# Windowed attention and a conformer layer on one Trainium2 core: half pages for the low parts of the output weights, and probability tiles in a pool of their own

## The chip, the cores and the metric

The kernel runs on one core of one Trainium2 chip. The metric is device time in microseconds (us) of one execution. The engines are named as the profile names them: PE (matrix multiply), DVE (vector), ACT (activation), POOL (GpSimd) and SP (the queue from which most DMAs are issued).

## The reference

Two layers on 1024 tokens of width 1024, with 256 context tokens, all in fp32. Layer A is windowed attention with a sink, layer B a conformer convolution. The change lies in the attention of layer A:

```python
for i in range(DEPTH):                       # 0: attention, 1: conformer convolution
    shift, scale, gate = split(silu(c) @ ada_w[i] + ada_b[i])
    h = rmsnorm(x, norm_g[i]) * (1 + scale) + shift
    if i % 2 == 0:
        q, k, v, z = split(h @ w_in)         # 16 q heads, 4 k/v heads of 128; q, k rotated
        kc, vc = split(h_ctx @ w_in[:, q_end:v_end])
        # per head and block of 128 queries: 3 blocks of 128 keys, 256 context keys, a sink
        s = concat([sink, q @ kc.T, q @ k_window.T]) * HEAD_DIM ** -0.5
        p = softmax(s)
        o = p_ctx @ vc + p_win @ v_window
        y = (o * silu(z)) @ w_out
    else:
        y = conformer_conv_branch(h, ...)    # GLU, depthwise conv of 31, layernorm, swish, gate
    x = x + gate * y
return rmsnorm(x, final_g)
```

## The kernel before, in words

Every fp32 operand of a matrix product is held as a high part (rounded to the matmul format) and a low part (the rest), and a product is three matmuls: high by high, low by high, high by low. ACT makes the high part by a copy, DVE or POOL the low part by a subtraction (`split_lo`). Names end in `h`/`hi` and `l`/`lo`.

Memory on the chip is 45 pages of 1024 words per partition and 6 half pages of 528 words (class `Pages`). A page is taken from the head of a list of free pages and put back at its end, so each tile lands on whichever page came free longest ago. The first instruction that writes a page's new tile waits for the last users of the old one.

The program is written as one sequence; a scheduler then sets the order of each engine's instructions by simulating them. PE's instructions are kept in program order from the start of attention. All compute instructions are issued through one helper (`InOrder.call`), so the profile shows them all on line L90 (in the listing of the changed kernel the same helper is L102).

Attention is a list of 128 steps, (h, qb) for 16 heads and 8 blocks of queries; step i = 8h + qb. In one step PE does: `scores` of step i+2 (into PSUM tile `pss`), some 11 to 15 matmuls of projections as filling (`fill`, PSUM tile `psg`), at some steps `pv` (into `pso`), and the `transposes` of step i (again a `pss`). Around them:

- `scores(h, qb)`: POOL copies the sink (`nsink`) into one column of a probability tile `p`, DVE adds the mask and takes the maximum in one custom instruction (`p<-pss,mask,nsink`, shown as CUSTOM_DVE_ANT_0 in the profile and ISA in an order), ACT takes the exponential, DVE the reciprocal, POOL scales. `p` is a whole page and three are live at a time.
- `transposes(h, qb)`: ACT copies the transposed probabilities to `pthi`, DVE subtracts to get `ptlo`; both are single tiles that `pv` reads after every fourth step.
- The projections' weights come through `WStream`: a load to `wraw` on SP, `whi` on ACT, `wlo` mostly on DVE. The rotation of q and k (`rope_start`, `rope_end`) multiplies by cosine and sine, and swaps the two halves of the head with two DMAs in between (on SP at the start of attention, on ACT later). At the start of attention (the code ahead of `steps`) rotated tiles of the first heads, the context's k and v (`kvc`) and the first `scores` overlap.
- `low_parts()`: the low parts of the two output weights (Wo of attention, Wp of layer B) are made once and stored to DRAM (`wolA`, `wolC`) for later. Before: 32 items of 512 KB on a page, each in three calls (load; first half: `lhi` on ACT into a half page, subtraction on POOL in place; second half likewise, then a store), one call per step.
- `adag` streams rows of the modulation weights (`dww_raw`, `wsum_raw`) which DVE accumulates into `mask_page`.
- At step (15,1) of the program the out-projection begins (the scheduler places parts of it earlier): loads of the attention's output `ozf` and of `wo` and `wol` through SP, split into `ozh`, `ozl`, `woh` on ACT and DVE.
- After heads 3, 7 and 11 the k and v of the next group are made between two steps ("regroup").

## Time and profile before

| | us |
|---|---|
| three runs of the kernel | 1745.61, 1746.29, 1748.8 |
| their median | 1746.29 |
| profiled execution, its own time | 1744.99 |
| its span, first to last instruction | 1743.2 |
| PE busy in the span | 1723.9 |
| DVE busy | 1151.1 |
| ACT busy | 868.2 |
| POOL busy | 853.5 |

The profiled execution is one more execution than the three runs; it is 1.3 us below their median, and its time is 1.8 us over its span. PE is busy in 99% of the span. So the views to read are those that show the few stretches in which PE waits, and what the other engines do in them: the list of PE's waits, then timelines of single engines there. Attention runs from 94.88 us (first `scores`) to some 840 us.

### The profile page before, as it was taken

What the parts mean: (1) busy time and instruction counts of PE and PEld (TensorE: products, weight loads), DVE (VectorE), ACT (ScalarE), POOL (GpSimd) and SP (SyncE); (2) the same over time, 40 slices, a digit from 0 to 9 for tenths busy, and PEclk for the clock granted to TensorE, in tenths of its full rate; (3) what the DMA queues carried; (4) which work ended last, traced back from release to release, by engine and by line L of the source; (5) the groups of instructions that cost most, each with busy time, mean ns of one, the idle gap of its engine ahead of it and who ended that gap; (6) DMA issues with size and microseconds to landing.
All of it is one profiled execution on the core that took longest, in us unless ns stands there. A gap on an engine that the chain in (4) does not pass through costs nothing.

```text
span 1743.2 us, 23901 instructions
## 1 busy us (share of the span) xinstructions
PE 1723.9 (99%) x8471; PEld 1424.9 (82%) x8471; DVE 1151.1 (66%) x2094; ACT 868.2 (50%) x1417; POOL 853.5 (49%) x797
## 2 busy tenths in 40 slices
PE   9999999999999999999999999999999999999998
PEld 5788888888888888887888888888888888887886
DVE  4676663666366654556215189999999999877912
ACT  5544443455344543446234355664665564466731
POOL 0135553655355543552001267998898888131410
PEclk9999999999999999999999999999999999999999
DMA  9334533454335443437776723020121202377971
GB/s 316 110 85 138 155 120 93 134 158 136 88 119 159 153 140 94 121 107 262 247 254 220 251 85 97 13 61 25 46 76 37 91 31 79 121 264 243 325 260 49
DMA packets 195324, 242.46 MB, mean 139 GB/s; under 512 B 11798, under 2 KB 126790, under 8 KB 195204
## 3 DMA queue, kind: packets, MB, share of 16 engines
q1 hardware_dynamic: 188692, 230.81, 40.6%
q10 hardware_dynamic: 6512, 10.11, 2.5%
q8 instruction: 67, 1.10, 0.3%
q14 instruction: 53, 0.43, 0.1%
HBM read 188.70 MB, written 41.69 MB: 132 GB/s over the span
## 4 chain that ended last, share of the span: by engine, by line
PE 91%; DMA 3%; DVE 3%; ACT 1%; issue 1%; POOL 1%; ACTq 0%; SPq 0%; DVEq 0%; POOLq 0%
PE psg L90 46%; PE pss L90 23%; PE pso L90 22%; DMA rope_half<-rope_half 1%; POOL rope_half L90 1%; DVE mask_page L90 1%; DVE ptlo L90 0%; DMA wo_page<-in_conv_w_out_dram 0%; DMA ozf_page<-ozd 0%; DMA wsum_raw<-in_ada_w_dram 0%; DMA wolC<-low_page 0%; DMA low_page<-in_conv_w_out_dram 0%; DVE p_page L90 0%; DVE x_page L90 0%; DMA rope_page<-rope_page 0%
## 5 line engine op out<-in xcount | busy, mean ns | idle before, releaser
L90 POOL TENSOR_TENSOR odd_half<-odd_half,prod_half 128x513 f32<-128x513 f32 (+2 forms) x252 | 313.2, 1251 | 23.8 <-ACT prod_half L90 10.5
L90 PE MATMUL psg<-hh_page,whi_page 128*128 128x512 f32 x608 | 240.7, 396 | 0.2 <-DVE kvc_page L90 0.2
L90 PE MATMUL psg<-hh_page,wlo_page 128*128 128x512 f32 x608 | 239.7, 394 | 0.0
L90 PE MATMUL psg<-hl_page,whi_page 128*128 128x512 f32 x608 | 239.4, 394 | 0.0
L90 ACT ACTIVATE prod_half<-ubuf,dww 128x513 f32<-128x513 f32 (+2 forms) x252 | 165.1, 674 | 110.6 <-POOL odd_half L90 108.4
L90 POOL TENSOR_SCALAR p_page<-p_page,sc 128x640 f32<-128x640 f32 (+1 forms) x128 | 109.3, 854 | 178.4 <-DVE sc L90 177.2
L90 PE MATMUL psg<-h2h_page,whi_page 128*128 128x512 f32 x464 | 183.8, 396 | 0.0
L90 PE MATMUL psg<-h2l_page,whi_page 128*128 128x512 f32 x464 | 182.5, 393 | 0.0
L90 PE MATMUL psg<-h2h_page,wlo_page 128*128 128x512 f32 x464 | 182.5, 393 | 0.0
L90 DVE SCALAR_TENSOR_TENSOR pss<-ubuf,dww,pss 128x512 f32<-128x512 f32 (+3 forms) x270 | 172.4, 671 | 0.1
L90 DVE SCALAR_TENSOR_TENSOR pss<-ubuf,wsum,pss 128x512 f32<-128x512 f32 (+3 forms) x270 | 171.8, 671 | 0.2
L90 ACT ACTIVATE p_page<-p_page,sc 128x641 f32<-128x641 f32 (+1 forms) x128 | 103.1, 806 | 129.9 <-DVE sc L90 114.9
L90 DVE TENSOR_TENSOR ptlo<-pss,pthi 128x640 fp32r<-128x640 f32 (+1 forms) x144 | 103.1, 716 | 62.0 <-ACT pthi L90 61.6
L90 ACT ACTIVATE pthi<-pss 128x640 fp32r<-128x640 f32 (+1 forms) x144 | 88.9, 617 | 103.4 <-PE pss L90 95.2
L90 PEld LDWEIGHTS psg<-hh_page,wlo_page 128*128 128x128 f32 x608 | 114.2, 188 | 24.0
L90 PEld LDWEIGHTS psg<-hh_page,whi_page 128*128 128x128 f32 x608 | 114.3, 188 | 23.0 <-DVE kvc_page L90 0.4
L90 PEld LDWEIGHTS psg<-hl_page,whi_page 128*128 128x128 f32 x608 | 114.3, 188 | 21.4
L90 POOL TENSOR_TENSOR wlo_page<-wraw_page,whi_page 128x1024 fp32r<-128x1024 f32 x35 | 87.9, 2514 | 86.6 <-ACT whi_page L90 70.2
L90 PE MATMUL pso<-h2h_page,whi_page 128*128 128x512 f32 x304 | 119.7, 394 | 0.0
L90 ACT ACTIVATE whi_page<-wraw_page 128x1024 fp32r<-128x1024 f32 x88 | 92.4, 1050 | 54.3 <-PE psg L90 25.3
L90 PE MATMUL pso<-h2h_page,wlo_page 128*128 128x512 f32 x304 | 119.5, 393 | 0.0
L90 PE MATMUL pso<-h2l_page,whi_page 128*128 128x512 f32 x304 | 119.4, 393 | 0.0
(265 smaller groups left out, 4111.1 us busy)
## 6 DMA issues: line engine op xcount, KB each, us to landing
wraw_page<-in_conv_w_in_dram SPq DMA_DIRECT2D x48, 512.0 KB
wraw_page<-in_attn_w_in_dram SPq DMA_DIRECT2D x40, 512.0 KB
wo_page<-in_attn_w_out_dram SPq DMA_DIRECT2D x32, 512.0 KB
wol_page<-wolA SPq DMA_DIRECT2D x32, 512.0 KB
wo_page<-in_conv_w_out_dram SPq DMA_DIRECT2D x32, 512.0 KB
wol_page<-wolC SPq DMA_DIRECT2D x32, 512.0 KB
rope_half<-rope_half ACTq DMA_DIRECT2D x72, 128.0 KB
araw_page<-in_ada_w_dram SPq DMA_DIRECT2D x32, 256.0 KB
```

What stands on the lines that cost most here:

```text
L90: r = f(*a, **k)
```

## The change

1. The pages become 42 pages and the same 6 half pages for the whole kernel, and a region of three more pages that changes its use twice. Until attention it is three "front" pages, which are given first to the short-lived tiles named in `BRIEF` (among them the rotation's `rope` tiles). Just ahead of `scores(0, 0)` it becomes three tiles of 642 words, for `p` alone, and two more half pages. After attention it is three pages again ("back"). A tile in the new pools waits for the tiles that lay there before.
2. `low_parts` has 64 items of 256 KB in half pages. An item is loaded two calls before it is split and stored; a call is made at two of three steps.
3. `WStream.load` makes no load in attention when no page is free. At a regroup the old k is freed before the new k is made, and one more weight load is asked for.

```diff
@@ -29,6 +29,7 @@
 SCALE = HD ** -0.5
 NEG = -1.0e30
 TB = T // P
+BRIEF = ("araw", "x", "junk", "hf", "rope", "arow")
 
 ADA_FP = ((0, 0), (0, 1), (0, 2), (0, 3), (1, 0), (1, 1), (2, 0), (2, 1))
 ADA_G = ()
@@ -55,26 +56,37 @@
 class Pages:
 
 
-    def __init__(self, pool, n, tag, words):
-        self.pool, self.tag, self.words = pool, tag, words
-        self.free_ = deque(range(n))
+    def __init__(self, tag, words):
+        self.tag, self.words = tag, words
+        self.free_ = deque()
+        self.first = deque()
         self.at = {}
         self.count = 0
 
+    def add(self, pool, n, tag, first=False):
+        slots = [(pool, f"{tag}{i}", first) for i in range(n)]
+        (self.first if first else self.free_).extend(slots)
+        return slots
+
+    def drop(self, slots):
+        for slot in slots:
+            (self.first if slot[2] else self.free_).remove(slot)
+
     def alloc(self, dt, shape=None, name="pg"):
-        if not self.free_:
+        own = self.first if name in BRIEF and self.first else self.free_ or self.first
+        if not own:
             raise RuntimeError(str([t[1].name for t in self.at.values()]))
-        i = self.free_.popleft()
+        slot = own.popleft()
         self.count += 1
-        t = self.pool.tile([P] + list(shape or [self.words]), dt, tag=f"{self.tag}{i}",
-                           name=f"{name}_{self.tag}_{self.count}", bufs=1)
-        self.at[id(t)] = (i, t)
+        t = slot[0].tile([P] + list(shape or [self.words]), dt, tag=slot[1],
+                         name=f"{name}_{self.tag}_{self.count}", bufs=1)
+        self.at[id(t)] = (slot, t)
         return t
 
     def free(self, *ts):
         for t in ts:
-            i, _ = self.at.pop(id(t))
-            self.free_.append(i)
+            slot, _ = self.at.pop(id(t))
+            (self.first if slot[2] else self.free_).append(slot)
 
 
 class InOrder:
@@ -112,8 +124,22 @@
     pgpool = ctx_stack.enter_context(tc.tile_pool(name="pages", bufs=1))
     ps = ctx_stack.enter_context(tc.tile_pool(name="ps", bufs=2, space=PSUM))
     dr = ctx_stack.enter_context(tc.tile_pool(name="dr", bufs=1, space=bass.MemoryType.DRAM))
-    pg = Pages(pgpool, 45, "page", 1024)
-    hp = Pages(pgpool, 6, "half", 528)
+    pg, hp, pp = Pages("page", 1024), Pages("half", 528), Pages("prob", 642)
+    pg.add(pgpool, 42, "page")
+    hp.add(pgpool, 6, "half")
+    stage = [None, []]
+
+    def swap(name, *kinds):
+        if stage[0] is not None:
+            for pages, slots in stage[1]:
+                pages.drop(slots)
+            stage[0].close()
+        stage[0] = ExitStack()
+        pool = stage[0].enter_context(tc.tile_pool(name=name, bufs=1, reuse_waits="tile"))
+        stage[1] = [(pages, pages.add(pool, n, f"{name}{k}", first)) for k, (pages, n, first) in enumerate(kinds)]
+        ctx_stack.callback(lambda s=stage[0]: s.close())
+
+    swap("front", (pg, 3, True))
 
     uid = [0]
 
@@ -215,7 +241,7 @@
             self.lo_eng = lo_eng or (lambda i: V)
 
         def load(self):
-            if self.nl >= len(self.srcs) or self.nl - self.ns >= self.nraw:
+            if self.nl >= len(self.srcs) or self.nl - self.ns >= self.nraw or behind and not pg.free_:
                 return
             i = self.nl
             r = pg.alloc(F32, [KT, P], "wraw")
@@ -729,22 +755,23 @@
 
     def low_parts():
 
-        items = [(pair_rows(w, m, kk), d[m, kk]) for w, d in ((Wo, wolA), (Wp, wolC)) for m in range(2) for kk in range(NK)]
-        for src, dst in items:
-            raw = pg.alloc(F32, [2, 512], "low")
-            SY.dma_start(out=raw, in_=src)
-            yield "open"
-            for b in range(2):
+        items = [(w[kk * 256 + e * P:kk * 256 + e * P + P, m * 512:m * 512 + 512], d[m, kk, :, e])
+                 for w, d in ((Wo, wolA), (Wp, wolC)) for m in range(2) for kk in range(NK) for e in range(2)]
+        got, held = deque(), []
+        for i in range(len(items) + 2):
+            if i >= 2:
+                raw, dst = got.popleft()
                 hi = hp.alloc(F32R, None, "lhi")
-                after(act(hi[:, 0:512], raw[:, b], AF.Copy), anchor_exp)
-                after(split_lo(G, raw[:, b], raw[:, b], hi[:, 0:512]), anchor_scale)
-                hp.free(hi)
-                if b == 0:
-                    yield "open"
-            SY.dma_start(out=dst, in_=raw)
-            pg.free(raw)
-            yield "shut"
-
+                after(act(hi[:, 0:512], raw, AF.Copy), anchor_exp)
+                after(split_lo(G, raw, raw, hi[:, 0:512]), anchor_scale)
+                SY.dma_start(out=dst, in_=raw)
+                hp.free(hi, held.pop(0))
+            if i < len(items):
+                held.append(hp.alloc(F32, None, "low"))
+                raw = held[-1][:, 0:512]
+                SY.dma_start(out=raw, in_=items[i][0])
+                got.append((raw, items[i][1]))
+            yield
 
 
     subs = [(h, m) for h in range(2) for m in range(2)]
@@ -1044,7 +1071,7 @@
         for n, (a, b) in enumerate(((0, 0), (0, 1), (1, 0))):
             PE.matmul(s[:, w0:512], q[a][:, qsl], kk[b][:, ksl], start=n == 0, stop=n == 2)
             PE.matmul(s[:, 512:768], q[a][:, qsl], c[:, b], start=n == 0, stop=n == 2)
-        p = pg.alloc(F32, [1024], "p")
+        p = pp.alloc(F32, None, "p")
         sc8 = small([P, 3], name="sc", bufs=6)
         nmx, l0, ri = (sc8[:, i:i + 1] for i in range(3))
         w = nw + CT
@@ -1076,7 +1103,7 @@
             PE.transpose(tb[:, rel * P:(rel + 1) * P], p[:, (kb - k0) * P:(kb - k0 + 1) * P], ident)
         for i in range(2):
             PE.transpose(tb[:, (3 + i) * P:(4 + i) * P], p[:, (nb + i) * P:(nb + i + 1) * P], ident)
-        pg.free(p)
+        pp.free(p)
         tv = tb[:, 0:640].rearrange("p (a b) -> p a b", b=P)
         for r0, r1 in (((0, 2), (3, 5)) if qb == 0 else ((1, 5),) if qb == TB - 1 else ((0, 5),)):
             b0 = 1 + ql + 4 * r0
@@ -1143,6 +1170,7 @@
     fill(6)
     tails[0]()
     fill(3)
+    swap("prob", (pp, 3, False), (hp, 2, False))
     scores(0, 0)
     tails[1]()
     fill(3)
@@ -1152,7 +1180,6 @@
     fill(4)
     steps = [(h, qb) for h in range(NH) for qb in range(TB)]
     lows = low_parts()
-    lstate = ["shut"]
     pvq = deque()
     for _ in range(2):
         next(adag)
@@ -1170,8 +1197,8 @@
             for _ in range(EA + 1):
                 next(projA)
             fillq.append((("wo", 0), early_proj()))
-        if lstate[0] == "open" or h and (h % 4 < 3 or qb < LOWS):
-            lstate[0] = next(lows, "shut")
+        if h and (h % 4 < 3 or qb < LOWS) and i % 3:
+            next(lows, None)
         nxt = steps[i + 1] if i + 1 < len(steps) else None
         regroup = nxt and nxt[1] == 0 and nxt[0] % 4 == 0
         ahead = steps[i + 2] if i + 2 < len(steps) else None
@@ -1186,11 +1213,13 @@
         if regroup:
             g = nxt[0] // 4
             old = kvt[g - 1]
+            pg.free(*old[0:2])
             run(job(("k", g)))
             transposes(h, qb)
             run(job(("v", g)))
             pv(h, 1)
-            pg.free(*old)
+            pg.free(*old[2:])
+            wsA.load()
             scores(*nxt)
             vlate.pop(g)()
             scores(*ahead)
@@ -1200,6 +1229,7 @@
             pvq.append((h, qb // 4))
         for _ in range(2 if qb == 1 or qb == 6 and h % 2 else 1):
             next(adag, None)
+    swap("back", (pg, 3, False))
     while pvq:
         fill(12)
         pv(*pvq.popleft())
```

PE's order is the same in both kernels, 7739 rows. SP has 681 rows for 616: 64 more DMAs. The orders of DVE, ACT and POOL differ in the attention alone.

**DVE at the start of attention.** Here `rope_page` with `cos` and `sin` (`_page_59x`, `_60x`) are parts of the rotation, `ql` the low part of the rotated q, `vl` of v, and the rows with `ISA p` are the mask and maximum of step (0,0). Before:

```order
L90 TENSOR_TENSOR ql_page_837<-rope_page_796,qh_page_836 128x512
L90 TENSOR_TENSOR rope_page_892<-rope_page_892,rope_page_891 128x512
L90 TENSOR_TENSOR rope_half_901<-pss_158,cos_page_599 128x512
L90 TENSOR_TENSOR vl_page_839<-pso_955,vh_page_838 128x512
L90 ISA p_page_972,sc_973<-pss_965,mask_page_819,nsink 128x512
L90 ISA sc_973 128x1
L90 TENSOR_TENSOR ql_page_837<-rope_page_892,qh_page_836 128x512
L90 TENSOR_TENSOR rope_half_900<-rope_half_900,sin_page_600 128x512
L90 TENSOR_TENSOR vl_page_839<-pso_979,vh_page_838 128x512
```


Now:

```order
L102 TENSOR_TENSOR ql_page_840<-rope_page_799,qh_page_839 128x512
L102 TENSOR_TENSOR vl_page_842<-pso_958,vh_page_841 128x512
L102 TENSOR_TENSOR rope_page_895<-pss_161,cos_page_602 128x512
L102 TENSOR_TENSOR rope_page_894<-rope_page_894,sin_page_603 128x512
L102 TENSOR_TENSOR vl_page_842<-pso_986,vh_page_841 128x512
L102 TENSOR_TENSOR rope_page_895<-rope_page_895,rope_page_894 128x512
L102 TENSOR_TENSOR rope_half_904<-pss_161,cos_page_602 128x512
L102 TENSOR_TENSOR kvc_page_838<-pso_996,kvc_page_838 128x256
L102 SCALAR_TENSOR_TENSOR zs_page_845<-zs_page_845,psg_848 128x512
L102 TENSOR_TENSOR ql_page_840<-rope_page_895,qh_page_839 128x512
L102 TENSOR_TENSOR rope_half_903<-rope_half_903,sin_page_603 128x512
L102 ISA p_prob_979,sc_980<-pss_972,mask_page_822,nsink 128x512
```


The mask and maximum of (0,0) stood four rows behind the first `ql` and ahead of the second `ql` and the second `vl`; now it stands eleven rows behind, after both of these, a `kvc` and a `zs`.

**SP there.** These are DMAs of one queue; the rows with 64x512 x2 are the rotation's swaps of halves. Before:

```order
L90 DMA wraw_page_843<-in_attn_w_in_dram 128x8x128
L90 DMA rope_half_788<-rope_half_787 64x512 x2
L90 DMA rope_page_795<-rope_page_794 64x512 x2
L90 DMA wraw_page_1015<-in_attn_w_in_dram 128x8x128
L90 DMA rope_page_891<-rope_page_890 64x512 x2
L90 DMA rope_half_900<-rope_half_899 64x512 x2
```


Now:

```order
L102 DMA wraw_page_846<-in_attn_w_in_dram 128x8x128
L102 DMA rope_half_791<-rope_half_790 64x512 x2
L102 DMA rope_page_798<-rope_page_797 64x512 x2
L102 DMA wraw_page_1022<-in_attn_w_in_dram 128x8x128
L102 DMA wraw_page_1184<-in_attn_w_in_dram 128x8x128
L102 DMA rope_page_894<-rope_page_893 64x512 x2
L102 DMA rope_half_903<-rope_half_902 64x512 x2
```


Two weight loads now stand ahead of the second swap of `rope_page`, before there was one.

**ACT at steps (15,0) and (15,1).** The two `pthi` here are the two parts of step (15,0), `p` the exponentials of later steps. Before:

```order
L90 ACTIVATE woh_page_7966<-wo_page_7910 128x1024
L90 ACTIVATE p_page_7779,sc_7780<-p_page_7779,sc_7780 128x641
L90 ACTIVATE ozh_page_8085<-ozf_page_8010 128x1024
L90 ACTIVATE pthi<-pss_7826 128x2x128
L90 ACTIVATE ozh_page_8014<-ozf_page_7964 128x1024
L90 ACTIVATE pthi<-pss_7826 128x2x128
L90 ACTIVATE p_page_7862,sc_7863<-p_page_7862,sc_7863 128x641
```


Now:

```order
L102 ACTIVATE woh_page_8069<-wo_page_8013 128x1024
L102 ACTIVATE ozh_page_8071<-ozf_page_8017 128x1024
L102 ACTIVATE p_prob_7882,sc_7883<-p_prob_7882,sc_7883 128x641
L102 ACTIVATE ozh_page_8117<-ozf_page_8067 128x1024
L102 ACTIVATE woh_page_8218<-wo_page_8180 128x1024
L102 ACTIVATE ozh_page_8252<-ozf_page_8216 128x1024
L102 ACTIVATE pthi<-pss_7929 128x2x128
L102 ACTIVATE p_prob_7965,sc_7966<-p_prob_7965,sc_7966 128x641
L102 ACTIVATE pthi<-pss_7929 128x2x128
```


Five splits of out-projection operands (two `woh`, three `ozh`) now stand ahead of the first `pthi`; before there were one `woh` and one `ozh`, and a second `ozh` between the two `pthi`.

## Rows read from the trace of the kernel before

**Rows 1.** Page, part 1: busy time, share of the span, instructions.

```profile
PE 1723.9 (99%) x8471; PEld 1424.9 (82%) x8471; DVE 1151.1 (66%) x2094; ACT 868.2 (50%) x1417; POOL 853.5 (49%) x797
```

**Rows 2.** Page, part 4: the chain that ended last, by engine.

```profile
PE 91%; DMA 3%; DVE 3%; ACT 1%; issue 1%; POOL 1%; ACTq 0%; SPq 0%; DVEq 0%; POOLq 0%
```

**Rows 3.** Waits of PE: engine tile <- releaser: total us, times, longest.

```profile
PE pso L90 <- DVE ptlo L90: 2.1, 5, 0.8
...
PE pso L90 <- ACT pthi L90: 1.3, 2, 0.8
PE pss L90 <- DVE ptlo L90: 0.9, 1, 0.9
PE pso L90 <- DVE mask_page L90: 0.9, 1, 0.9
PE psg L90 <- DVE zs_page L90: 0.8, 1, 0.8
PE psg L90 <- DVE rope_half L90: 0.7, 1, 0.7
```

**Rows 4.** Timeline of PE, first steps: start, us, instruction [idle before <-releaser].

```profile
96.08 0.39 PE L90 MATMUL pss<-kh_page,ql_page 128*128 128x256 f32 x1 [0.56 <-DVE ql_page L90]
...
100.66 0.34 PE L90 MATMUL pss<-kh_page,qh_page 128*128 128x384 f32 x1
```

**Rows 5.** Timeline of DVE, first steps of attention.

```profile
89.22 0.69 DVE L90 TENSOR_TENSOR rope_half<-rope_half,sin_page 128x512 f32<-128x512 f32 x1 [0.96 <-DMA rope_half<-rope_half]
...
92.09 0.68 DVE L90 TENSOR_TENSOR rope_page<-rope_page,rope_page 128x512 f32<-128x512 f32 x1
...
94.73 0.69 DVE L90 TENSOR_TENSOR rope_page<-rope_page,sin_page 128x512 f32<-128x512 f32 x1 [1.16 <-DMA rope_page<-rope_page]
95.34 0.68 DVE L90 TENSOR_TENSOR ql_page<-rope_page,qh_page 128x512 fp32r<-128x512 f32 x1
...
97.74 0.74 DVE L90 CUSTOM_DVE_ANT_0 p_page<-pss,mask_page,nsink 128x512 f32<-128x512 f32 x1
...
98.41 0.69 DVE L90 TENSOR_TENSOR ql_page<-rope_page,qh_page 128x512 fp32r<-128x512 f32 x1
```

**Rows 6.** Timeline of SP, first steps: each row issues two DMAs.

```profile
86.21 1.16 SPq L90 DMA_DIRECT2D rope_half<-rope_half  x2
...
90.56 1.11 SPq L90 DMA_DIRECT2D rope_page<-rope_page  x2
```

**Rows 7.** Timeline of DVE at step (1,3).

```profile
161.25 2.06 DVE L90 TENSOR_TENSOR wlo_page<-wraw_page,whi_page 128x1024 fp32r<-128x1024 f32 x1
```

**Rows 8.** Timeline of POOL at step (1,3).

```profile
160.94 1.30 POOL L90 TENSOR_TENSOR low_page<-low_page,lhi_half 128x512 f32<-128x512 f32 x1 [0.46 <-ACT lhi_half L90]
162.19 2.25 POOL L90 TENSOR_TENSOR rope_half<-rope_half,sin_page 128x512 f32<-128x512 f32 x1
```

**Rows 9.** Timeline of DVE, steps (15,0) and (15,1).

```profile
812.84 1.23 DVE L90 TENSOR_TENSOR ozl_page<-ozf_page,ozh_page 128x1024 fp32r<-128x1024 f32 x1 [1.32 <-ACT ozh_page L90]
...
814.79 2.33 DVE L90 TENSOR_TENSOR ozl_page<-ozf_page,ozh_page 128x1024 fp32r<-128x1024 f32 x2
817.05 0.67 DVE L90 SCALAR_TENSOR_TENSOR zs_page<-zs_page,psg 128x512 f32<-128x512 f32 x1
```

**Rows 10.** Timeline of ACT, step (15,0).

```profile
811.74 1.07 ACT L90 ACTIVATE ozh_page<-ozf_page 128x1024 fp32r<-128x1024 f32 x1 [2.02 <-DMA ozf_page<-ozd]
```

**Rows 11.** Tile low_page: POOL durations (min/median/max), then what ACT idled for.

```profile
L90 POOL TENSOR_TENSOR low_page<-low_page,lhi_half x64: 1275/1295/2042, 145.0 to 752.3; 128x512 f32<-128x512 f32 x64
...
  DMA low_page<-in_conv_w_out_dram: 3.1, 1
...
  DMA low_page<-in_attn_w_out_dram: 0.7, 1
```

**Rows 12.** Waits of SP: total us, times, longest.

```profile
SPq L90 <- POOL low_page L90: 54.7, 21, 5.5
```

**Rows 13.** Waits of POOL: total us, times, longest.

```profile
POOL p_page L90 <- PE psg L90: 36.5, 10, 8.7
```

## The prediction

> **What bounds the kernel now.** I read the page's first part, then its chain, then the list of PE's waits, and last the timelines of single engines around the waits. PE is busy 1723.9 us of a span of 1743.2 [rows 1] and makes 91% of the chain that ended last [rows 2]. The change leaves PE's instructions and their order as they are, so it can act on the time only through PE's waits. Those that lie in attention and have a row of their own are few [rows 3]: 2.1 us for `ptlo` ahead of `pv`, 1.3 for `pthi`, 0.9 for a PSUM tile that `ptlo` still reads (at step (15,0)), 0.9 for `mask_page` and 0.8 for `zs` (both just behind it, where the out-projection begins), 0.7 for a rotated tile at a regroup, and 0.56 for the first `ql` [rows 4]. They come to 7.3 us. That is the ceiling of any gain, 0.4% of the time. A loss has no ceiling. From no change a measurement of this kernel can tell about 0.2%, 3.5 us: half of all these waits would have to go for the change to be seen as faster.
>
> **What costs nothing.** Low parts: the work is the same, 64 subtractions on POOL of 1.295 us (median) and as many copies on ACT. Their loads now come two calls ahead instead of one, but ACT idled for the old loads 3.1 + 0.7 = 3.8 us in all [rows 11], and ACT is busy half the time [rows 1]; what hides it is PE's filling, and there is nothing on the path to win. SP issues 64 DMAs more, at some 0.55 us each (1.11 for two [rows 6]): 35 us in 700, on a queue that mostly waits. The rule that skips a weight load when no page is free does not act as long as a page is free, and the three pages are replaced by the three tiles of 642 words that would have used them. The swap back at the end stands behind the last `p`. The sum goes against the profiled execution of 1744.99 us; the median of the three runs, 1746.29, is 1.3 above it, and I add the sum to the median.
>
> **The start of attention, +1.4 us.** All rotated tiles of q now come from the three front pages, so the second rotation (q hi) takes the memory of the first (q lo), and its swap can be issued only when the first rotation's sum has read it. Before, that sum ran at 92.09 (0.68 us) and the second swap had already been issued at 90.56 [rows 5, 6]. So the second swap now goes at 92.8 at the earliest; it has two weight loads ahead of it in SP's queue, too, where it had one, so I take 93.3. From issue to the sine product that waits for it, the two swaps with a row took 3.0 us (86.21 to 89.22) and 4.2 us (90.56 to 94.73) [rows 5, 6]; the middle, 3.6, gives 96.9. From there DVE runs, in the order printed above: sine product, `vl`, sum, cosine product of k hi, `kvc`, `zs`, `ql`, sine product, and only then the mask and maximum of (0,0). Seven of these at 0.6 us from start to start (94.73 to 95.34 [rows 5]) and one of half that width at 0.33 (an estimate: half the width) make 4.5 us: 101.4, and 0.7 more for the instruction itself (97.74 to 98.41 [rows 5]): 102.1. Before it ran at 97.74. PE's `scores` of (0,2) uses the PSUM tile that this instruction reads, and began at 100.66 [rows 4]; now 102.1, **+1.4 us**. The wait of 0.56 for the first `ql` goes, since `ql` now follows its sum at once, but that is time PE then spends waiting here: it is inside the difference and is not subtracted again. With the earliest issue and the faster swap the same sum gives 92.8 + 3.0 + 4.5 + 0.7 = 101.0, +0.3; with 93.8 and 4.2 it gives 103.2, +2.5.
>
> Who else waits: POOL's first copy into a new `p` tile waits for the q-hi sum, as its memory is a front page. Behind it on POOL are the scalings of (0,0) and of the next steps, but the copy is ready before the maximum is, so it does not add.
>
> **Step (1,3), -0.8 us.** The longest wait for `ptlo` is 0.8 us [rows 3]. There DVE ran a `wlo` of 2.06 us just ahead of `ptlo` [rows 7], where an operation of the same width (`ozl`) takes 1.23 [rows 9]; POOL ran the subtraction of a low part (1.30 us) and a product of the rotation (2.25 us) at the same time [rows 8]. In the new order this `wlo` stands ahead of a rotation product and a maximum, so it is done before `ptlo` can be asked for, and ACT has no `lhi` there. I take the whole wait as gone; the other end is that nothing goes. The Trainium skill (SBUF — State Buffer, Who interferes with whom) says that a DVE operation with two inputs in SBUF and a POOL operation that reads SBUF hold a port against each other, the second waiting out the first. The 2.06 us row agrees; by that rule the rotation's product on POOL, which stays, could still block the `wlo`, and this term would be 0.
>
> At (1,7), (9,3) and (9,7) what stands ahead of `ptlo` on DVE is unchanged, and those waits stay. At (2,7) a copy goes from ACT, but `ptlo` is still behind a `wlo`: 0.
>
> **The start of the out-projection, -0.6 us.** Three waits, 0.9, 0.9 and 0.8 [rows 3]. DVE had an `ozl` of 1.23 us ahead of the second `ptlo` of (15,0) and two, 2.33 us, ahead of the `zs` that ended the 0.8 [rows 9]. All three now stand elsewhere, so the 0.8 goes. But ACT now has three `ozh` and two `woh` ahead of the first `pthi` of (15,0). In the old order the last `ozh` there waited for its load until 811.74 [rows 10]. If the last one still has to, `pthi` comes at 812.8, an exponential and the second `pthi` follow, and the second `ptlo` ends about when it did: that 0.9 stays, or grows by a microsecond. The wait for `mask_page` I leave. At (15,3) three `ozl` (3 x 1.23 us) now stand ahead of `ptlo`; PE asks for that at the end of the step, so it costs 0 to 2. Ends: -2.6 (all three waits gone) and +2; I take **-0.6**, nearer to the first, because the `zs` is the one piece that the order settles.
>
> **The middle.** 128 `p` tiles come from three slots in turn instead of a list of pages; the copy that opens a tile waited for PE up to 8.7 us, 36.5 in all [rows 13], with no wait of PE behind it. Now it waits for the transposes of three steps before, which PE does before the scores that the tile is for. SP waits for a low part on POOL before each store: 54.7 us in 21 waits [rows 12], now 64 stores for 32. What is behind a store on SP are loads for steps to come. I cost both at 0, ±1.5.
>
> Sum: 1.4 - 0.8 - 0.6 + 0 = 0.0. **Forecast: 1746.3 us, no change that can be told**, own range 1742.8 to 1749.8.
>
> **Rivals.**
> *Faster.* The front pages cost nothing (+0.3), the whole of the three waits of the out-projection goes (-2.6), (1,3) goes (-0.8), and the regroup loses its 0.7 [rows 3]: -3.8, 1742.5. For it: the `ozl` are indeed out of DVE's way. Against it: five splits on ACT in front of `pthi`. Chance 0.13.
>
> *Slower: the swap behind two loads.* The swap with no load just ahead took 3.0 us, the one with a load of 512 KB issued 1 us before it took 4.2 [rows 5, 6]. If each load ahead adds 1.2, two make it 5.4; from 93.8 that gives 99.2, the maximum ends at 104.4, and `scores` of (0,2) starts 3.7 us late. From 3.5 on (a swap that lands after 99.0) it alone is over the bound if (1,3) and the out-projection give nothing back; with the out-projection's other end, +0.7, it is +4.4: 1750.7. For it: both loads do stand ahead in the queue. Against: they may have been issued long before. Chance 0.2.
>
> *It does nothing at all.* The waits of PE at other places are hidden behind its filling, the start has slack that I don't see, the reordering moves waits about: 0, 1746.3. It shares the forecast's bounds, and I give it 0.17 of the 0.67 there.
>
> *Many small transfers.* The Trainium skill (DMA: Bandwidth & Descriptors, Bandwidth) asks for transfers of 1 MiB or more and counts about 2 us of fixed time for each; by that, 64 more of half the size would be an estimated 128 us of transfer time more. On the path that is nothing unless a load that DVE needs falls behind a store on SP. As a mechanism here: one store that waits the longest seen, 5.5 us [rows 12], ahead of a modulation row, makes DVE late by up to a step's slack; three such, at 0.9 each as the one wait for `mask_page` in the trace [rows 3], give 2.7: 1749.0, within the forecast's range.
>
> **Numbers.** The forecast and the rival that nothing happens hold 0.67 between 1742.8 and 1749.8 (within 0.2%), the faster case 0.13, the slower 0.2. To leave out no more than 2 in 10 the range reaches to the centres of both outer cases: 1742.5 to 1750.7.
>
> **What would show it.** In the profile of the changed kernel: DVE's CUSTOM of (0,0) at 101 to 102.5 instead of 97.74, and a PE wait for it of 1 to 3 us ahead of the scores of (0,2), in place of the 0.56 for `ql`; the swap's issue on SP after 92.8. At some 164 us no wait for `ptlo`; near 815 a wait for `ptlo` of about 0.9, none for `zs`. PE busy unchanged at 1724. The forecast is wrong if PE's waits in attention add up to less than 4 or more than 11 us, above all if waits appear in the middle, at steps that had none.

## The result, and the profile after

The changed kernel takes 1759.78 us (median of 4 runs, 1758.51 to 1762.68); the kernel before takes 1745.95 beside it (4 runs). The ratio is 1.0083, with a 95% interval of 1.0067 to 1.0098: slower by 0.8%, 14 us. The forecast was no change, 1746.3, and the range to 1750.7; both were wrong. The span of the profiled execution grew from 1743.2 to 1757.0 us, by 13.8.

The first part of the page after, to be read beside [rows 1], says that no engine has more work, but that PE is busy for longer:

```profile
PE 1728.2 (98%) x8471; PEld 1429.0 (81%) x8471; DVE 1149.9 (65%) x2094; ACT 866.3 (49%) x1417; POOL 850.8 (48%) x797
```

PE's busy time grew by 1728.2 - 1723.9 = 4.3 us for the same 8471 matmuls. The list of PE's waits of the changed kernel (total us, times, longest), to be read beside [rows 3]:

```profile
PE pso L102 <- DVE ptlo L102: 7.8, 7, 2.0
PE pso L102 <- ACT pthi L102: 4.6, 4, 2.4
...
PE pss L102 <- DVE ptlo L102: 1.2, 1, 1.2
```

Waits ahead of `pv` for `ptlo` and `pthi` came to 2.1 + 1.3 = 3.4 us, and now come to 7.8 + 4.6 = 12.4. By place, from the timelines of PE (us of wait):

| place | before | after |
|---|---|---|
| first `scores` (up to 105 us) | 0.7 | 2.4 |
| ahead of `pv` at (0,7) | 0 | 3.1 |
| (1,3) | 0.8 | 0 |
| (1,7) | 0.3 | 3.9 |
| (2,7) | 0.9 | 1.7 |
| (3,3) | 0 | 0.7 |
| (9,3), (9,7) | 1.4 | 0.9 |
| regroup behind (11,7) | 0.9 | 1.4 |
| (14,3) | 0 | 1.5 |
| out-projection, (15,0) to (15,3) | 2.6 | 1.8 |
| sum | 7.6 | 17.4 |

So PE waits 9.8 us more, and the bulk of that, 7.5, lies in one place that repeats three times: ahead of `pv` at the end of heads 0, 1 and 2 (3.1, 3.5 and 0.8 more). Here is the first of them, rows of several engines' timelines of the changed kernel in order of time (start, us, instruction, idle before it and its releaser):

```profile
127.92 0.38 SPq L102 DMA_DIRECT2D wraw_page<-in_attn_w_in_dram  x1
...
129.83 0.33 SPq L102 DMA_DIRECT2D low_half<-in_attn_w_out_dram  x1
...
130.26 0.38 SPq L102 DMA_DIRECT2D wraw_page<-in_attn_w_in_dram  x1
...
130.42 1.12 ACTq L102 DMA_DIRECT2D rope_half<-rope_half  x2
...
138.71 1.28 POOL L102 TENSOR_TENSOR rope_half<-rope_half,sin_page 128x512 f32<-128x512 f32 x1 [3.97 <-PE psg L102]
139.93 0.19 POOL L102 COPY p_prob<-nsink 128x1 f32<-128x1 f32 x1
...
141.40 0.63 ACT L102 ACTIVATE qh_page<-rope_half 128x512 fp32r<-128x512 f32 x1 [5.40 <-POOL rope_half L102]
...
144.17 0.58 ACT L102 ACTIVATE pthi<-pss 128x512 fp32r<-128x512 f32 x1
...
144.81 0.49 PE L102 MATMUL pso<-pthi,kvc_page 128*128 128x512 f32 x1 [1.08 <-ACT pthi L102]
...
147.31 0.50 PE L102 MATMUL pso<-ptlo,kvc_page 128*128 128x512 f32 x1 [2.01 <-DVE ptlo L102]
```

Two weight loads of 512 KB went out at 127.92 and 130.26, with a load of a low part (256 KB) between them and one of modulation rows behind. The rotation's swap for the next q, two DMAs of 128 KB on ACT's queue, was issued at 130.42, in the midst of them. The sine product on POOL, which needs the swapped data, began at 138.71, 8.3 us after the issue. (The releaser that the row names, a `psg`, is no input of it; the same row in four runs below names the swap's DMA.) The copy `qh` on ACT waited 5.40 us for the sum behind that product, and behind it in ACT's order stand the exponential of step (1,1), `whi` and `pthi` of (0,7). That exponential was late for a second reason: it reads the column that POOL copies from the sink (counted in order, the copy at 139.93), and this copy stands on POOL behind the sine product. So it could have begun at 140.12, and `qh` held it until 141.93. `pthi` began at 144.17 and PE waited 1.08 us for it, and 2.01 more for `ptlo`, which stands on DVE behind the `wlo` of that same `whi` and behind a maximum that before came after it (0.80 of the 2.01). The same place before, with one weight load, issued after the swap:

```profile
126.35 0.18 POOL L90 COPY p_page<-nsink 128x1 f32<-128x1 f32 x1 [0.34 <-PE pss L90]
...
129.66 1.12 ACTq L90 DMA_DIRECT2D rope_half<-rope_half  x2
...
130.41 0.38 SPq L90 DMA_DIRECT2D wraw_page<-in_attn_w_in_dram  x1
...
133.11 1.28 POOL L90 TENSOR_TENSOR rope_half<-rope_half,sin_page 128x512 f32<-128x512 f32 x1 [2.74 <-DMA rope_half<-rope_half]
...
136.35 0.63 ACT L90 ACTIVATE qh_page<-rope_half 128x512 fp32r<-128x512 f32 x1 [1.23 <-POOL rope_half L90]
...
139.31 0.58 ACT L90 ACTIVATE pthi<-pss 128x512 fp32r<-128x512 f32 x1
```

There the sine product came 3.45 us after the issue, `qh` waited 1.23 us, `pthi` began at 139.31 and PE never waited. The copy for (1,1) had been done at 126.35, ahead of the swap: the probability tile was a page from the long list then, and is now one of three. At (1,7) of the changed kernel the picture is the same: a pair of weight loads at 173.3 and 173.9 us, a swap at 176.24 that took 7.6 us (5.3 in the kernel before, behind one load of 512 KB), ACT idle for 6.2 ahead of `qh`, the copy for (2,1) at 185.05 behind the sine product (170.60 before). At (2,7) there is a pair, too, at 219.0 and 220.6, but the swap at 221.68 took 5.8 us, and in the kernel before it took 6.4, behind two loads of low parts of 512 KB each. So a slower swap is not what made the 0.8 more of wait there; on POOL the subtraction of a low part (229.60, 1.29 us) now stands between the sine product and the sum.

The rest of the loss comes with the clock. The table of windows of the changed kernel (window, us, busy time and instructions of PE, PEld, DVE, ACT and POOL, then the granted clock of TensorE, DMA share, GB/s):

```profile
190.00:195.00 5.00, 3.08 (x11) 2.44 (x12) 2.83 (x7) 1.83 (x4) 3.69 (x4) 0.83 0.44 119
195.00:200.00 5.00, 5.00 (x28) 4.79 (x27) 2.25 (x5) 0.92 (x3) 0.18 (x1) 0.83 0.31 117
235.00:240.00 5.00, 3.56 (x13) 2.88 (x14) 2.36 (x6) 1.85 (x5) 2.24 (x3) 0.77 0.08 26
240.00:245.00 5.00, 5.00 (x28) 4.70 (x28) 2.71 (x6) 1.38 (x3) 0.19 (x1) 0.89 0.27 105
800.00:805.00 5.00, 4.98 (x21) 4.66 (x22) 1.67 (x3) 2.25 (x4) 0.80 (x1) 0.66 0.10 30
```

Behind the waits at (1,7), (2,7) and (14,3) the granted clock falls to 0.83, 0.77, 0.66 on the mean of 5 us; matmul by matmul it is the lower level, 1.2 GHz, for some 3.4 us, in which a matmul of 256 columns takes 213 ns from start to start where it takes 118 otherwise. Each time PE had waited 1.5 to 3.9 us shortly before. Five us times the missing share (0.17 + 0.17, 0.23 + 0.11, 0.34) is 1.7 us lost each time, 5.1 in all. Waits and clock, 9.8 + 5.1, more than cover the 13.8; the rest, -1.1, is small differences elsewhere, half of it a wait of 0.5 at 1611 us that this execution does not have. The kernel before had no such fall of the clock until its last 10 us. The profiled execution lost least of the four: its mean granted clock is 0.996, that of the others 0.994, 0.994 and 0.992, where the profiled one before has 0.998. So in the median run the clock's part is larger, an estimated 7 us (0.998 less 0.994, of 1757 us), half of the loss.

The start went as worked out. Rows of the changed kernel there, to be read beside [rows 4 to 6]:

```profile
93.44 1.11 SPq L102 DMA_DIRECT2D rope_page<-rope_page  x2
...
96.39 0.69 DVE L102 TENSOR_TENSOR rope_page<-rope_page,sin_page 128x512 f32<-128x512 f32 x1 [0.44 <-DMA rope_page<-rope_page]
...
98.93 0.44 PE L102 MATMUL pss<-kh_page,qh_page 128*128 128x384 f32 x1 [1.54 <-DVE rope_half L102]
...
100.93 0.74 DVE L102 CUSTOM_DVE_ANT_0 p_prob<-pss,mask_page,nsink 128x512 f32<-128x512 f32 x1
...
101.83 0.41 PE L102 MATMUL pss<-kh_page,qh_page 128*128 128x384 f32 x1 [0.84 <-DVE sc L102]
```

The second swap was issued at 93.44 (the prediction took 93.3), its sine product began at 96.39 (96.9), the maximum of (0,0) at 100.93 (101.4), and `scores` of (0,2) at 101.83 (102.1) where it had begun at 100.66. Only the wait came in two parts: 0.84 there, and 1.54 one step sooner, ahead of `scores` of (0,1), for the cosine product of k hi, which reads the PSUM tile that they go into.

### The profile page after: what moved, and what is told of

Same layout as the page of the kernel before. It is cut to its first block, busy times and chain, and to the rows that moved or that the text cites. A ratio compares the mean times of both kernels' runs of the same rounds, so it can differ in the third digit from the quotient of the medians.

```text
span 1757.0 us, 24166 instructions
## 1 busy us (share of the span) xinstructions
PE 1728.2 (98%) x8471; PEld 1429.0 (81%) x8471; DVE 1149.9 (65%) x2094; ACT 866.3 (49%) x1417; POOL 850.8 (48%) x797
## 4 chain that ended last, share of the span: by engine, by line
PE 73%; DMA 3%; POOL 2%; DVE 1%; issue 1%; ACT 1%; ACTq 0%; POOLq 0%; DVEq 0%; SPq 0%
PE psg L102 37%; PE pso L102 18%; PE pss L102 18%; DMA rope_half<-rope_half 1%; POOL rope_half L102 1%; DMA wo_page<-in_attn_w_out_dram 1%; DMA wsum_raw<-in_ada_w_dram 0%; POOL p_prob L102 0%; POOL low_half L102 0%; DVE p_prob L102 0%; DVE ptlo L102 0%; DVE mask_page L102 0%; POOL ql_page L102 0%; DVE x_page L102 0%; ACT pthi L102 0%
## 5 line engine op out<-in xcount | busy, mean ns | idle before, releaser
L102 POOL TENSOR_SCALAR p_prob<-p_prob,sc 128x640 f32<-128x640 f32 (+1 forms) x128 | 104.4, 815 | 199.0 <-DVE sc L102 192.2
L102 ACT ACTIVATE p_prob<-p_prob,sc 128x641 f32<-128x641 f32 (+1 forms) x128 | 103.0, 805 | 132.6 <-DVE sc L102 108.3
```

The lines of the kernel that those rows point to most:

```text
L102: r = f(*a, **k)
```

## The experiments

Theory A: with the probability tiles out of the one list of pages, two successive weight loads inherit the two pages of a finished head's q, which come free in the same instant, so the loads go out together just ahead of a swap; the swap is late, and ACT, standing in order at `qh`, makes `pthi` late. Theory B: the low parts' 64 smaller loads and stores do it. Theory C: what the start loses is carried on. The ratios are each to the kernel before beside it; the changed kernel's is 1.0083.

One detail of theory A, which stands in the expectations, is to be corrected first. The semaphores that the loads wait for show that the pages of a pair are at heads 0 to 2 not both those of q: one had held `ql` of the finished head, the other the `whi` of a weight just used up, and their last readers on PE are seven matmuls apart. Only from the pair at 264.5 and 265.0 us on are both pages those of q, with neighbouring matmuls. What follows for the loads is nearly the same: they are released within 2 us of each other.

**Where the weight loads' pages come from.** One edit to the changed kernel:

```diff
-        slot = own.popleft()
+        slot = own.pop() if name == "wraw" else own.popleft()
```

> The changed kernel, with one edit: a weight load (wraw) takes the page that was freed last, instead of the one freed longest ago, which is mostly the page that the split just before has given back. Theory A (pairs: without the probability tiles in the list of pages, two weight loads inherit the two pages of a finished head's q, freed in the same instant, so 2 x 512 KB go out together just ahead of the rotation's swap, which lands 4 to 5 us late; ACT stands in order at the copy qh that waits for it, and pthi, ptlo and PE's pv are late): the loads come singly, some 20 us apart, the swaps at the heads 1 to 3 take 3 to 5 us, PE's waits of 144 to 237 us (8.7 us) and the lower clock behind them (some 4 us) go: 1746 to 1749 us. Theory B (the 64 smaller loads and stores of the low parts, two calls ahead, are what the swap waits for): unchanged, 1757 or more. Theory C (what the start of attention loses is carried through the steps): unchanged, 1757 or more.

Measured: 1749.44 us, ratio 1.0031 (1.0019 to 1.0042): of the 0.83% lost, 0.52% came back. The weight loads go out singly, and at (0,7) none is near the swap; the next is at 141.71. Timelines at the place of the rows above:

```profile
129.99 0.33 SPq L102 DMA_DIRECT2D low_half<-in_attn_w_out_dram  x1
...
131.00 1.12 ACTq L102 DMA_DIRECT2D rope_half<-rope_half  x2
...
134.13 1.29 POOL L102 TENSOR_TENSOR rope_half<-rope_half,sin_page 128x512 f32<-128x512 f32 x1 [2.08 <-DMA rope_half<-rope_half]
...
137.38 0.64 ACT L102 ACTIVATE qh_page<-rope_half 128x512 fp32r<-128x512 f32 x1 [0.82 <-POOL rope_half L102]
...
141.71 0.38 SPq L102 DMA_DIRECT2D wraw_page<-in_attn_w_in_dram  x1
```

The sine product comes 3.1 us after the issue, with a low part's load right ahead of it, and `qh` waits 0.82. PE has no wait at (0,7) and (1,7); at (2,7) 0.9 stay, and 0.7 ahead of scores at 223. The time lay a little above the upper end of what A had expected (1749). Theories B and C fall as the main cause; what stays of the loss is the start (2.3 us of waits), (14,3) (2.4 us of waits, and behind them the lower clock, 0.72 and 0.60 on the mean of 785 to 790 and 790 to 795 us, 3.4 us lost in this execution) and waits that the new order put elsewhere.

**Each half of the change alone.** The new low parts on the kernel before (`low_parts` of the changed kernel, 44 pages and 8 half pages, a call at two of three steps), and the changed kernel with the old low parts (its probability tiles, front pages and weight loads at the regroups as they are):

```diff
-    swap("prob", (pp, 3, False), (hp, 2, False))
+    swap("prob", (pp, 3, False), (lp, 1, False))
...
-            raw = pg.alloc(F32, [2, 512], "low")
+            raw = lp.alloc(F32, [2, 512], "low")
```

> The kernel before, with the new low parts alone (64 items in half pages, two calls ahead, two of three steps); 44 pages and 8 half pages, the probability tiles still on pages. Theory A: the probability tiles still turn the list of pages over, weight loads come singly: 1744 to 1749 us, no new waits of PE ahead of pv at (0,7), (1,7), (2,7). Theory B: 1755 or more.

> The changed kernel with the low parts as before (32 items of 512 KB, three calls each, one call per step), on one page of their own in the region of the probability tiles; no extra half pages. Theory A: the probability tiles are out of the list, the weight loads still come in pairs: 1755 to 1763 us, with swaps of 6 us or more at the first heads. Theory B: 1745 to 1749.

Measured: low parts alone 1749.12, ratio 1.0026 (1.0016 to 1.0036); probability tiles with the old low parts 1755.9, ratio 1.0063 (1.0051 to 1.0075). So the larger share does not need the new low parts, as A has it, and the pair of weight loads is there, at some 128.5 and 130.1 us. Rows of that run at (0,7):

```profile
131.00 1.12 ACTq L102 DMA_DIRECT2D rope_half<-rope_half  x2
...
137.60 1.30 POOL L102 TENSOR_TENSOR rope_half<-rope_half,sin_page 128x512 f32<-128x512 f32 x1 [5.54 <-DMA rope_half<-rope_half]
...
140.89 0.63 ACT L102 ACTIVATE qh_page<-rope_half 128x512 fp32r<-128x512 f32 x1 [4.30 <-POOL rope_half L102]
...
146.80 0.68 PE L102 MATMUL pso<-ptlo,kvc_page 128*128 128x512 f32 x1 [2.01 <-DVE ptlo L102]
```

6.6 us for the swap, 4.30 for `qh`, and the wait of PE for `ptlo` is there. But the low parts alone are not free; their time is a shade above the most that A had expected (1749). Weight loads came singly, no wait at (0,7) or (2,7), and yet 4.7 us were lost. In that run's list of PE's waits there are three that the kernel before does not have, or not so long:

```profile
PE pss L90 <- DVE sc L90: 2.1, 2, 1.5
...
PE psg L90 <- DVE zs_page L90: 1.8, 1, 1.8
PE pss L90 <- DVE kl_page L90: 1.3, 1, 1.3
```

They lie at the start (1.3 ahead of a `kl` at 106), at 388 and 582 us, and where the out-projection begins (1.8 for `zs`), with the lower clock behind the last (0.50 in 820 to 825 us). What makes them stays open: no run takes them apart.

**Pairs without low parts near.** The changed kernel with the low parts begun at head 3:

```diff
-        if h and (h % 4 < 3 or qb < LOWS) and i % 3:
+        if h > 2 and (h % 4 < 3 or qb < LOWS) and i % 3:
```

> The changed kernel with the low parts begun at head 3 instead of head 1; what is left of them at the end is done in one go ahead of the out-projection, so the total time is not the question here, the first heads are. At heads 0 and 1 only weight loads (in pairs) and the modulation rows stand near the swaps. Theory A: the pair is enough: the swaps at some 130 and 176 us still take 6 to 8 us, and PE still waits 2 us or more ahead of pv at (0,7) and at (1,7). If the low parts' loads are needed for it: swaps of 3 to 5 us and no waits of over 0.9 us there.

Its time (one run) is 1751.24 us against 1745.28. At (0,7):

```profile
128.90 2.00 SPq L102 DMA_DIRECT2D wraw_page<-in_attn_w_in_dram  x2
...
131.39 1.11 ACTq L102 DMA_DIRECT2D rope_half<-rope_half  x2
...
138.02 1.29 POOL L102 TENSOR_TENSOR rope_half<-rope_half,sin_page 128x512 f32<-128x512 f32 x1 [5.58 <-DMA rope_half<-rope_half]
...
141.30 0.63 ACT L102 ACTIVATE qh_page<-rope_half 128x512 fp32r<-128x512 f32 x1 [4.33 <-POOL rope_half L102]
...
147.22 0.71 PE L102 MATMUL pso<-ptlo,kvc_page 128*128 128x512 f32 x1 [2.00 <-DVE ptlo L102]
```

With only the pair and a load of modulation rows near it the swap takes 6.6 us, and PE waits 2.0; at (1,7) it takes 6.9, and PE waits 0.5 + 2.0. In the changed kernel, with low parts beside the pair, these were 8.3 and 7.6 us, 3.1 and 3.9 us of wait. So the pair is enough for the wait, and with the low parts it is 1.1 and 1.4 us longer (one execution). The clock falls behind (0,7) in this run (the row as in the table of windows), and not behind (1,7) and (2,7):

```profile
145.00:150.00 5.00, 3.00 (x9) 2.30 (x9) 2.72 (x7) 0.92 (x2) 1.00 (x2) 0.73 0.09 26
```

**Pairs made in the kernel before.** The loads go out two at a time, and nothing else is edited:

```diff
+        def load(self):
+            if behind and self.nl > self.ns:
+                return
+            for _ in range(2 if behind else 1):
+                self.load_one()
```

> The kernel before, with one edit: in attention WStream.load makes no load while one is waiting to be split, and then makes two. Low parts, pages and probability tiles are as before; only the weight loads now go out two at a time. Theory A (the pair makes the rotation's swap late, ACT waits in order for qh): 1749 to 1756 us, with swaps of 5 to 8 us behind the pairs and waits of PE for pthi or ptlo ahead of pv at (0,7), (1,7) or (2,7). Theory B (low parts) or C (start): as before, 1743 to 1746.

Measured: 1744.72, ratio 0.9997 (0.9988 to 1.0005), no change. This was a miss, and it makes the theory narrower. Rows at (0,7):

```profile
129.18 0.38 SPq L90 DMA_DIRECT2D wraw_page<-in_attn_w_in_dram  x1
...
129.90 1.12 ACTq L90 DMA_DIRECT2D rope_half<-rope_half  x2
...
130.65 0.38 SPq L90 DMA_DIRECT2D wraw_page<-in_attn_w_in_dram  x1
...
135.68 1.29 POOL L90 TENSOR_TENSOR rope_half<-rope_half,sin_page 128x512 f32<-128x512 f32 x1 [1.66 <-DMA rope_half<-rope_half]
...
137.29 0.83 ACT L90 ACTIVATE p_page<-p_page,sc 128x641 f32<-128x641 f32 x1 [1.93 <-DVE sc L90]
...
139.07 0.61 ACT L90 ACTIVATE qh_page<-rope_half 128x512 fp32r<-128x512 f32 x1
...
140.06 0.59 ACT L90 ACTIVATE pthi<-pss 128x512 fp32r<-128x512 f32 x1
```

The swap took 5.8 us between its two loads, longer than the 3.45 of the kernel before, but here the scheduler had put `qh` behind the exponential and `whi`: it idled for nothing, and `pthi` began at 140.06. At (1,7) and (2,7) the pairs stood off the swaps, which took 3.5 and 4.6 us. Two more things differ from the changed kernel: the second load went out behind the swap here, and the copy for (1,1) was done at 122.76, so POOL's order could not hold the exponential. The run shows that a pair costs nothing by itself; which of these differences saved it, it does not tell apart.

**The link on ACT.** The changed kernel, pairs and all, with `qh` of heads 0 to 2 behind `pthi`:

```diff
-        act(dh, r, AF.Copy)
-        split_lo(rest, dl, r, dh)
...
+        def end():
+            ins = act(dh, r, AF.Copy)
+            after(ins, anchor_hi)
+            split_lo(rest, dl, r, dh)
...
+        ends.append((len(seen), end))
```

> The changed kernel, pairs of loads and all, with the copy qh (and the subtraction for ql) of the rotated q in heads 0 to 2 put on ACT behind pthi of the step in which it stood ahead of it, two steps later in the program. Theory A: the swap is as late as in the changed kernel (6 to 8 us at the pairs), but pthi no longer stands behind qh; the three pairs of waits at 144 to 237 us (8.6 us) shrink to 3 or less, and the lower clock behind them goes: 1748 to 1752 us. If the wait of PE comes from POOL (the sine product ahead of the scaling) and not from ACT: 1756 or more.

Measured: 1762.82, ratio 1.0106 (1.0092 to 1.012): by its time it falls to the other reading, POOL (1756 or more). Rows at (0,7):

```profile
141.25 0.83 ACT L102 ACTIVATE p_prob<-p_prob,sc 128x641 f32<-128x641 f32 x1 [2.26 <-POOL p_prob L102]
...
143.50 0.59 ACT L102 ACTIVATE pthi<-pss 128x512 fp32r<-128x512 f32 x1
143.98 0.63 ACT L102 ACTIVATE qh_page<-rope_half 128x512 fp32r<-128x512 f32 x1
```

The swap took 7.2 us and `qh` stands behind `pthi`, yet `pthi` comes only 0.7 us sooner than in the changed kernel: the exponential ahead of it now waits for POOL's copy, which ended at 141.22 behind the sine product and the sum. PE did not wait there, and of the waits ahead of `pv` at (0,7), (1,7) and (2,7) only 0.6 at (1,7) is left; but at (0,7) PE asked for `pthi` 2.8 us later than in the changed kernel (146.55 against 143.73), mostly because it had waited for the `qh` and `ql` of the swap before. The edit had moved these for every swap of heads 0 to 2, the punctual ones too, and PE's next `scores` need them. The list of waits has two entries that the changed kernel does not have:

```profile
PE pss L102 <- POOL ql_page L102: 7.4, 3, 6.0
PE pss L102 <- ACT qh_page L102: 5.4, 3, 2.4
```

12.8 us lost anew, for 8.1 gone. So this run does not show that ACT's order is the link. What the rows show is that the late swap reaches `pthi` through POOL (sine product, copy, exponential) and through `qh` on ACT; the second can have cost 1.8 us at (0,7) of the changed kernel (140.12 to 141.93) and 0.4 in the two runs above with pairs, where the copy ended at 140.98 and 141.39. No run moves the copy.

**The start, and edits together.** The second rotation's tiles on ordinary pages (its `rope_start` under another name than those of `BRIEF`), alone, with the page freed last, and with that for attention only; and the page freed last together with `qh` behind `pthi`:

```diff
-    rq1 = rope_start(acc1[1], hi, pg, SY)
+    rq1 = rope_start(acc1[1], hi, pg, SY, "qrot")
```

> The changed kernel, with the tiles of the second rotation of q (q hi, at the start of attention) taken from the ordinary pages, not from the three front pages. Theory A: only the two waits at 98.9 and 101.8 us (1.5 + 0.8 us) shrink, to 0.7 together as before; the rest stays: 1757 to 1759 us. Theory C: most of the loss goes, 1750 or less.

> The changed kernel with a weight load on the page freed last, and the second rotation of q at the start on ordinary pages. Theory A: the sum of the two edits run singly: the loads come singly, and the start loses 1.9 us instead of 2.3: 1748 to 1750 us.

> The changed kernel with a weight load on the page freed last, and qh of heads 0 to 2 behind pthi. Theory A: with single loads the swaps are short and the place of qh matters little: within 1.5 us of the run with the page freed last alone, 1747 to 1750 us; its waits at 223 and 228 us (1.6 us) may go, since qh waited 6.6 and 4.4 us there.

> As the run with both edits (weight loads on the page freed last, second rotation of q on ordinary pages), but with the page freed last in attention alone, from step 3 to its end; ahead of it and in layer B the page freed longest ago, as before. The run with both edits had waits of 2.0 us between 1034 and 1059 us, in layer B, that neither kernel has. Theory A: these go, the rest stays: 1745 to 1747 us, level with the kernel before; the waits left in attention (about 1.2 at the start, 1.4 at 226, 0.8 at 248, 2.1 at 786) are those that the change still costs, against 2.6 won where the out-projection starts.

Measured: ordinary pages alone 1757.66, ratio 1.0073 (1.0058 to 1.0087); with the page freed last 1746.92, ratio 1.0013 (1.0004 to 1.0022); with that in attention only 1747.82, ratio 1.0019 (1.001 to 1.0028); page freed last and `qh` behind 1767.98, ratio 1.0136 (1.012 to 1.015). The first says that theory C is not it: the start's waits turn from 1.5 + 0.8 into 0.7 for a `ql` and 1.3 for a `vl`, and the loss of heads 0 to 2 stays. The second is the best version of the change, better than the 1748 to 1750 expected: 1.7 us short of the kernel before, where the change as it was is 13.8 short. The third missed its 1745 to 1747 and shows that the small waits in layer B did not cost what was put on them; its interval overlaps the second's. The fourth missed by 18 us what was expected (1747 to 1750): with the loads single, moving `qh` still costs that much, so it has a price that has nothing to do with late swaps.

**Two controls.** The page freed last in the kernel before, and the changed kernel without the weight load added behind a regroup:

```diff
-        i = self.free_.popleft()
+        i = self.free_.pop() if name == "wraw" else self.free_.popleft()
```

```diff
             pg.free(*old[2:])
-            wsA.load()
```

> The kernel before with that edit alone: a weight load takes the page freed last. Its loads come singly already. Theory A: no gain from it, 1744 to 1748 us (up to 2 us lost in layer B, as in the run with both edits). If taking the page freed last were good by itself, apart from the pairs: 1741 or less.

> The changed kernel without the weight load that was added behind a regroup. Theory A: the pairs of the first heads do not come from it and stay, with their waits: 1757 to 1761 us. If that load were what makes the pairs: 1750 or less.

Measured: 1746.22, ratio 1.0007 (0.9998 to 1.0016), so the page freed last does nothing by itself; and 1757.15, ratio 1.0073 (1.0059 to 1.0087), with the waits at heads 0 to 2 as before, so the pairs do not come from that load.

## Why the prediction was wrong, point by point

- **"The ceiling of any gain is 7.3 us, a loss has no ceiling."** Right, and it should have made the upper end of the range wider: the same sentence says that only waits that are not yet in the trace can hurt.
- **Start of attention, +1.4.** Right: 101.83 - 100.66 = 1.2 at `scores` of (0,2), by the steps named.
- **(1,3), -0.8.** Right: the wait is gone. The weighed alternative, that POOL's rotation product would still hold the `wlo` up, did not come about there.
- **Out-projection, -0.6.** Right in sum: 2.6 became 1.8. The wait for `zs` is gone, the one for `ptlo` at (15,0) grew from 0.9 to 1.2, and (15,3) has a new one of 0.6, as weighed. The one for `mask_page` (0.9), which the prediction left in, went as well; without that the term would have come out at about 0, so the size is in part luck.
- **"At (1,7), (9,3) and (9,7) what stands ahead of `ptlo` on DVE is unchanged, and those waits stay."** Wrong at (1,7), where 0.3 became 3.9. The rows ahead of `ptlo` were compared on DVE alone. `qh` had moved to the front of ACT's order there, and what it waits for, the swap, was not costed. At (0,7) ACT's order is the same in both kernels, and the wait came all the same, from the DMAs and POOL; DVE's order has a maximum ahead of `ptlo` that was behind it, 0.8 us. At (9,3) 0.3 became 0.9, and the 1.0 at (9,7) went. "At (2,7) ... 0" was 0.8 too low.
- **"The middle, 0, ±1.5."** This is the step that failed. It looked at the probability tiles' own waits and at SP's stores, and not at what else the list of pages gives its pages to. Taking 128 tiles out of the list changed which page each weight load gets, and so when SP may issue it. No term of the sum was about the time at which a weight load goes out. At the start the order of SP showed such a pair, and it was even priced; the swaps of the steps, on ACT's queue, were not set against one. And the copy that opens a tile was put at nothing because PE's transposes free its slot in time; that it now stands on POOL behind the sine product, and so waits for the swap, was not seen. In place of 0, ±1.5, the waits ahead of `pv` at (0,7), (1,7) and (2,7) grew by 7.5 us, with the pairs as the cause of most of it: single loads in the changed kernel brought back 0.52% of the 0.83%.
- **The sign of being wrong** came true as the prediction put it: PE's waits in attention add up to 17.4 us, above 11, with new ones at steps that had none; PE was busy for 1728.2 us and not 1724.
- **The clock** had no term. The 5.1 us behind the new waits are a third of the loss in the profiled execution.
- **The slower rival** named a pair of loads ahead of a swap, with the price of 1.2 us for each load, at the one place that it looked at. The mechanism was right, at other places, (0,7) and (1,7), and the price too low: it would make 5.4 of two loads; measured, with two and no low part near, are 6.6 and 6.9 us there, where the swap with no large load ahead of it took 3.45. At its own place it did not occur: the two loads had begun to go out 4 us earlier, and the swap took 3.0 us (93.44 to 96.39).
- **Many small transfers.** The Trainium skill (DMA: Bandwidth & Descriptors, Bandwidth) asks for transfers of 1 MiB or more. The trace has no sign that the size of the low parts' transfers is what counted: they come on top of a collision that two loads of 512 KB make. The low parts alone cost 0.26%, for reasons that no run took apart.

The wait at (14,3), 1.5 us and a fall of the clock, has another cause. There, too, a swap stands among loads (of `ozf` and `wo`), and the wait stayed in the runs with single weight loads; but the swap took 5.8 us in both kernels. What differs are the orders: on POOL the subtraction of a low part (793.20, 1.29 us) now stands between the sine product and the sum, which comes 9.1 us after the swap's issue where it came 7.9 after, and on DVE a maximum (798.34, 0.8 us) stands ahead of `ptlo` that was behind it. Together that is 2.1 us, enough for the wait; no run moves either.

## What to carry to other kernels

When tiles leave a common pool, the question is not only what they wait for in their new place but who inherits the pages that they used to take, and when those come free: an allocation order is a schedule of the loads into it. Look in the DMA queues for big transfers that now go out back to back, and set them against every small transfer that an in-order engine waits for. A small pool has a second price: the instruction that opens a tile comes later in its engine's order, and may now stand behind one that waits for a transfer. And for a wait on one engine compare the orders of all engines that feed it, not of the last one.

## What the runs showed of the hardware

Two DMAs of 128 KB took 3.0 to 3.5 us to the first instruction that used them at the places above with no large load issued just ahead, 6.0 to 6.9 us behind two loads of 512 KB from another queue that had gone out 2.5 and 0.9 us ahead (the run with the low parts begun late), and 8.3 with a load of 256 KB more among them. The kernel before has 6.4 behind two loads of 512 KB for low parts (at 212.89 us). Where the pair went out some 3 us ahead or more, the changed kernel has 4.0 to 5.1 (at 267.85, 455.51 and 648.09 us). Queues of two engines are no separate lanes here.

TensorE's granted clock fell to its lower level after some waits and not after others: behind 1.08 + 2.01 us at (0,7) of the changed kernel it stayed at 1.00, behind 2.38 + 1.48 at (1,7), 0.82 + 0.87 at (2,7) and 0.35 + 1.18 at (14,3) it fell for some 3.4 us. With the low parts begun late it was the other way round: it fell behind 2.00 at (0,7) and stayed at 1.00 behind 0.48 + 2.01 at (1,7). So the length of a wait alone does not tell what it costs.
